# Modulation columns fetched ahead in a two-block transformer kernel, with nine weight buffers, a norm through ones and a bias write from 128 partitions

## The chip, the cores and the metric

The kernel runs on one core of one Trainium2 chip. The metric is the device time of one execution in microseconds (us); the number that counts is the median of several executions.

## What is computed

Two blocks in a row on x of 256 tokens by 2048 channels, all in float32. The first one is modulated by a vector c: six vectors of 2048 (shift, scale and gate for the mixer and for the feed-forward) come from one product with a 2048 x 12288 matrix, `w_ada`.

```python
c_act = jax.nn.silu(c)
mod = c_act @ w_ada[l] + b_ada[l]
sh1, sc1, gt1, sh2, sc2, gt2 = jnp.split(mod, 6, axis=-1)
h = modulate(rms_norm(x, g_mix[l]), sh1, sc1)     # h * (1 + scale) + shift
z = h @ w_in[l]                                   # 2048 -> 11344 columns
...                                               # stick-breaking and top-k sparse attention, with rel_bias
x = x + gt1[:, None, :] * (merged @ w_out[l])
h = modulate(rms_norm(x, g_ffn[l]), sh2, sc2)
a = causal_dwconv(h @ w_gate[l], conv_w[l], conv_b[l])
y = (jax.nn.silu(a) * (h @ w_up[l])) @ w_down[l]
x = x + gt2[:, None, :] * y
```

The second block is gated linear attention and a SwiGLU feed-forward; the change touches it only through the number of weight buffers and one norm.

## The kernel before, in words

Activations are held transposed, 128 channels on the partitions and 256 tokens along the free axis, each as a pair `hi`, `lo` of shorter floats. Every dense layer streams its weights once from memory as **weight tiles** of 128x1024 floats (512 KB). `weights` (L85) takes a buffer `raw`, has SyncE (SP) issue the DMA (L89), lets ScalarE (ACT) round it to `hi` (L92) and VectorE (DVE) take the rest `lo = raw - hi` (L93). There are five `raw` and three `hi` and `lo` buffers. TensorE (PE) then multiplies: three matmuls of 256 columns per 128x128 piece in `mm3` (L120 to L122), 24 per tile, or two (512 and 256 columns) in `dense_b` (L110, L111).

**The modulation is not on TensorE.** `w_ada` is read in 96 **columns** of 128 outputs each, and a column is two `raw` buffers of 512 KB. `mod_col` (L189) issues both DMAs (L196) and has VectorE multiply each with `c_act` and sum along the free axis (L198). The columns share the five `raw` buffers and the SP queue with the weight tiles. Vectors `0` (shift) and `1` (scale) are needed before the first projection can be fed: row block k of h needs column k of both, then `h_mod` (L265 to L274) makes it.

**The first projection, `w_in_k`,** is therefore ordered with the contraction outermost (`batch`, L532): three batches b of 16 output tiles; a batch holds all eight PSUM banks and walks over row blocks k, two weight tiles per step k. Each batch runs in two parts, k from 0 to 6 and from 7 to 15. After the first part ScalarE copies the 16 sums out (L548), after the second VectorE adds them in (L550). `grow` (L525) makes one more row block of h, hence two columns; the function `ahead` says when: every step of the first part of batch 0, every second step later, until all 16 exist in the second part of batch 0. This first stage ends with `w_in_k`; then come `w_in_a` (32 tiles, L163 to L165), `w_in_b` (50), `w_o_dsa` (16), `w_o_sb` (16), `w_out` (32) and the feed-forward.

**The other 64 columns** are spread by a credit: every weight tile adds `self.rate`, and a full credit makes one `mod_step` (L201), fetch and reduction together. The rate is 0.36 from the last two parts of `w_in_k` to the end of `w_o_dsa`, 0 in `w_o_sb` and `w_out`, and 16 columns are left for the feed-forward.

**The first norm** squares x on ScalarE (L495), adds on VectorE (L498), sums over partitions by matmuls with one column each (L501), takes the root (L227) and reciprocal (L228) of 128x2 numbers, and `spread` (L230) brings them back to 128x256 by a diagonal, a matmul (L237) and a copy (L238). `stat_end` (L240) does the same for later norms.

**The bias** of the sparse attention: `rows` (L324) makes 8 rows of 383 numbers on 8 partitions and writes each 128 times to memory as `skew` (L329, 1532 KB); `head` (L332) reads it back with a stride, which shifts each row (L334).

Beside this dense work the attention's steps run from a list, one or two per weight tile (`pump`). A scheduler fixes the order on each engine when the program is built, and each engine and the SP queue works strictly in that order.

Of the kernel before, what the change touches and what calls it, by code (L numbers as in the profile page):

```python
# [32 lines left out]
class Core:  # L33
    def __init__(self, ctx, tc, ap):
# [10 lines left out]
        self.modq = deque()  # L45
        self.rate = self.credit = 0.0
# [38 lines left out]
    def weights(self, src, n):  # L85
# [103 lines left out]
    def mod_col(self, ci, j):  # L189
        nc = self.nc  # L190
        n = ci * KD + j
        m = self.mod[ci][:, j:j + 1]
        for hf in range(2):
            c = slice(hf * 1024, (hf + 1) * 1024)
            raw = self.wp.tile([P, 1024], F32, name="raw", tag="raw", bufs=5)
            nc.sync.dma_start(raw, self.ap["w_ada"][n, :, c])  # L196
            init = m if hf else self.vec["b_ada"][:, n:n + 1]
            nc.vector.tensor_tensor_reduce(out=raw, in0=raw, in1=self.c_act[:, c], scale=1.0, scalar=init,  # L198
                                           op0=ALU.mult, op1=ALU.add, accum_out=m)

    def mod_step(self, n=1):  # L201
        for _ in range(n):
            if self.modq:
                self.mod_col(*self.modq.popleft())

# [33 lines left out]

    def stat_end(self):  # L240
        nc = self.nc
        m = self.misc()
        nq = 4 if self.st_two else 2
        for i, st in enumerate((self.st, self.sq)):
            for q in range(nq):
                nc.tensor.matmul(m[:, q:q + 1], st[:, q * P:(q + 1) * P], self.ones[:, 0:1],
                                 start=(i == 0 and q == 0), stop=(i == 1 and q == nq - 1), skip_group_check=True)
# [4 lines left out]
        self.rs = self.alloc()  # L252
        r1, r2 = self.rs[:, :S], self.rs[:, S:]
        if not self.st_two:
            self.spread(r1, rt[:, :2])
            return r1
# [27 lines left out]
    def setup(self):  # L284
# [7 lines left out]
        self.c_act = self.big()  # L292
        nc.sync.dma_start(self.c_act[0:1, :], ap["c"])
        for i in range(4):
            c = slice(i * 512, (i + 1) * 512)
            m = self.misc()
            nc.tensor.matmul(m, self.ones[0:1, :], self.c_act[0:1, c], start=True, stop=True)
            nc.scalar.activation(self.c_act[:, c], m, AF.Silu)
        self.vec = {}
        off = 0  # L300
        nv = sum(w for _, w in VECS)
        vt = self.cp.tile([P, nv], F32, name="vecs")
        nc.sync.dma_start(vt, ap["vecs"])
        for n, w in VECS:
            self.vec[n] = vt[:, off:off + w]
            off += w
# [7 lines left out]
    # ---- constants of the attention  # L314
    def rel_bias(self):
# [5 lines left out]
        g = self.dp.tile([NH, P, 383], F32, name="skew")  # L321
        self.bias = [self.alloc() for _ in range(4)]

        def rows():  # L324
            m = self.misc()
            nc.tensor.matmul(m[:NH, :383], rb, oh[:32, :383], start=True, stop=True)
            e = self.scr(384)
            nc.scalar.copy(e[:NH, :383], m[:NH, :383])
            nc.sync.dma_start(g, e[:NH, :383].unsqueeze(1).broadcast_to([NH, P, 383]))  # L329
            self.free(oh)  # L330

        def head(h):  # L332
            src = g[h].rearrange("p q -> (p q)")[127:127 + P * 382].rearrange("(p q) -> p q", q=382)[:, :S]
# [143 lines left out]
    def mixer(self):  # L477
# [6 lines left out]
        self.load_consts()  # L484
        sh1, g1 = self.mod[0], self.mod[1]

        def mods(k):
            self.mod_col(1, k)
            self.mod_col(0, k)
            nc.vector.scalar_tensor_tensor(g1[:, k:k + 1], g1[:, k:k + 1], 1.0, self.vec["g_mix"][:, k:k + 1],  # L490
                                           op0=ALU.add, op1=ALU.mult)
        with self.tc.high_priority(offset=400):
            sq = [self.alloc() for _ in xs]
            for j, x in enumerate(xs):
                nc.scalar.activation(sq[j], x, AF.Square)  # L495
            for n in (4, 2, 1):
                for j in range(n):
                    nc.vector.tensor_add(sq[j], sq[2 * j] if n < 4 else sq[j], sq[2 * j + 1] if n < 4 else sq[j + 4])  # L498
            m = self.misc()
            for q in range(4):  # L500
                nc.tensor.matmul(m[:, q % 2:q % 2 + 1], sq[0][:, q * P:(q + 1) * P], self.ones[:, 0:1],  # L501
                                 start=(q == 0), stop=(q == 3), skip_group_check=True)
            self.free(*sq)
            rt = self.sp.tile([P, 4], F32, name="rt", tag="rt", bufs=2)
            self.rstd(rt[:, :2], m[:, :2], D)
            self.rs = self.alloc()
            r = self.rs[:, :S]
# [577 lines left out]
```

## Time and profile before

| | us |
|---|---|
| median of three executions | 2773.17 |
| fastest and slowest of them | 2756.18, 2775.2 |
| span of the profiled execution, first to last instruction | 2767.9 |
| TensorE busy in that span | 2672.7 |

The span stands 5.3 us under the median; which of the executions was profiled isn't told, so what lies around the span is known only as that difference. A profile row of instructions names the line, the engine, the operation, what it writes and reads, the shapes and the count, then busy time, the mean duration, and the idle time before. In a row of time the start comes first, then the duration, and in square brackets how long the engine had been idle and what ended that.

### The profile page before, as it was taken

To read this page: it belongs to the slowest core of one execution; us is meant where nothing else is said; L and a number is where in the kernel's file an instruction comes from. 1 tells how busy PE (TensorE), PEld (TensorE's weight loads), DVE (VectorE), ACT (ScalarE), POOL (GpSimd) and SP (SyncE) were. 2 spreads that over 40 slices of the span, in tenths; PEclk is the share of its full clock that TensorE was granted. 3 is DMA by queue.
4 is the path that set the end of the run, shared out by engine and by line. 5 is a ranking of instruction groups with operands and counts; after the bars stand their busy time and mean duration, and the time that the engine had idled before them with its cause. 6 is when DMAs were issued, how large, how long until landed. Compare 5 with 4: busy or idle time off the path is not lost.

```text
span 2767.9 us, 41793 instructions
## 1 busy us (share of the span) xinstructions
PE 2672.7 (97%) x16310; PEld 2370.0 (86%) x16310; DVE 1876.6 (68%) x2881; ACT 1307.5 (47%) x1929; POOL 0.2 (0%) x4
## 2 busy tenths in 40 slices
PE   6899995999999999999999999999999999999999
PEld 5889874998987888888888888888888888888888
DVE  7886785766768777777655568657766666665444
ACT  3443342554545444444444464445554444444433
POOL 0000000000000000000000000000000000000000
PEclk9999998999999999999999999999999999999999
DMA  8998886877755666666566644545555555556664
GB/s 306 313 327 276 290 270 186 283 240 253 238 190 180 227 221 227 232 216 218 183 181 190 185 158 144 159 152 176 188 184 191 191 189 190 191 190 186 195 204 148
DMA packets 167674, 585.70 MB, mean 212 GB/s; under 512 B 18576, under 2 KB 23408, under 8 KB 167474
## 3 DMA queue, kind: packets, MB, share of 16 engines
q1 hardware_dynamic: 167474, 583.03, 65.1%
q8 instruction: 127, 2.08, 0.3%
q14 instruction: 73, 0.59, 0.1%
HBM read 579.22 MB, written 3.67 MB: 211 GB/s over the span
## 4 chain that ended last, share of the span: by engine, by line
PE 76%; DMA 6%; DVE 4%; issue 2%; ACT 1%; SPq 0%; DVEq 0%; ACTq 0%
PE acc L110 44%; PE acc L111 22%; DMA raw<-in_w_ada 4%; DVE lo L93 2%; PE acc L122 1%; PE acc L120 1%; PE acc L121 1%; PE acc L163 1%; PE acc L164 1%; PE acc L165 1%; DMA raw<-in_w_in_b 1%; DVE raw L198 1%; PE misc L829 1%; DMA raw<-in_w_in_k 1%; ACT hi L92 0%
## 5 line engine op out<-in xcount | busy, mean ns | idle before, releaser
L110 PE MATMUL acc<-slot,hi 128*128 128x512 f32 x5056 | 1775.4, 395 | 1.0 <-DVE t L175 1.0
L93 DVE TENSOR_TENSOR lo<-raw,hi 128x1024 fp32r<-128x1024 f32 (+1 forms) x916 | 1102.9, 1206 | 673.4 <-ACT hi L92 668.5
L92 ACT CAST hi<-raw 128x1024 fp32r<-128x1024 f32 (+1 forms) x916 | 947.0, 1035 | 1217.9 <-issue 544.5
L111 PE MATMUL acc<-slot,lo 128*128 128x256 f32 x5056 | 1420.9, 281 | 0.0
L110 PEld LDWEIGHTS acc<-slot,hi 128*128 128x128 f32 x5056 | 949.2, 188 | 225.2 <-issue 1.5
L111 PEld LDWEIGHTS acc<-slot,lo 128*128 128x128 f32 x5056 | 952.3, 188 | 1.1 <-issue 0.8
L120 PE MATMUL acc<-slot,hi 128*128 128x256 f32 x1056 | 304.5, 290 | 53.5 <-ACT hi L92 49.5
L122 PE MATMUL acc<-slot,lo 128*128 128x256 f32 x1056 | 297.5, 289 | 9.7 <-DVE lo L93 9.1
L121 PE MATMUL acc<-slot,hi 128*128 128x256 f32 x1056 | 300.0, 286 | 0.0
L120 PEld LDWEIGHTS acc<-slot,hi 128*128 128x128 f32 x1056 | 204.0, 193 | 57.7 <-ACT hi L92 52.5
L122 PEld LDWEIGHTS acc<-slot,lo 128*128 128x128 f32 x1056 | 201.2, 194 | 13.8 <-DVE lo L93 13.7
L198 DVE CUSTOM_DVE_ANT_0 raw<-raw,big,vecs 128x1024 f32<-128x1024 f32 x96 | 123.2, 1284 | 125.1 <-DMA raw<-in_w_ada 124.8
L121 PEld LDWEIGHTS acc<-slot,hi 128*128 128x128 f32 x1056 | 204.2, 193 | 0.4 <-DVE slot L273 0.3
L198 DVE CUSTOM_DVE_ANT_0 raw<-raw,big,mod 128x1024 f32<-128x1024 f32 x96 | 123.1, 1283 | 9.6 <-DMA raw<-in_w_ada 8.2
L122 PE MATMUL misc<-slot,lo 128*128 128x256 f32 x384 | 108.2, 282 | 2.5 <-DVE lo L93 2.5
L120 PE MATMUL misc<-slot,hi 128*128 128x256 f32 x384 | 108.5, 283 | 1.6 <-DVE slot L550 1.6
L121 PE MATMUL misc<-slot,hi 128*128 128x256 f32 x384 | 108.2, 282 | 0.0
L163 PE MATMUL acc<-hi,slot 128*128 128x512 f32 x256 | 103.2, 403 | 1.6 <-ACT hi L92 1.3
L164 PE MATMUL acc<-lo,slot 128*128 128x512 f32 x256 | 102.1, 399 | 2.1 <-DVE lo L93 2.1
L165 PE MATMUL acc<-hi,slot 128*128 128x512 f32 x256 | 101.2, 395 | 0.0
L175 DVE TENSOR_TENSOR t<-acc,t 128x256 f32<-128x256 f32 x188 | 78.6, 418 | 0.3
L174 ACT COPY t<-acc 128x256 f32<-128x256 f32 x209 | 76.0, 364 | 1.1 <-PE acc L146 1.1
(223 smaller groups left out, 1744.4 us busy)
## 6 DMA issues: line engine op xcount, KB each, us to landing
raw<-in_w_gu SPq DMA_DIRECT2D x344, 512.0 KB, 3.7
raw<-in_w_ada SPq DMA_DIRECT2D x192, 512.0 KB, 5.4
raw<-in_w_in_k SPq DMA_DIRECT2D x96, 512.0 KB, 5.7
raw<-in_w_down SPq DMA_DIRECT2D x80, 512.0 KB, 4.3
raw<-in_w_dn SPq DMA_DIRECT2D x80, 512.0 KB, 4.5
raw<-in_gla_b SPq DMA_DIRECT2D x66, 512.0 KB, 3.6
raw<-in_w_in_b SPq DMA_DIRECT2D x50, 512.0 KB, 4.8
raw<-in_w_in_a SPq DMA_DIRECT2D x32, 512.0 KB, 4.5
```

What stands on the lines that cost most here:

```text
L92: self.mark = nc.scalar.copy(hi[:, :n], raw[:, :n])
L93: nc.vector.tensor_sub(lo[:, :n], raw[:, :n], hi[:, :n])
L110: nc.tensor.matmul(acc, hi[:, w], x, start=(k + j == 0), stop=False, skip_group_check=True)
L111: nc.tensor.matmul(acc[:, 1], lo[:, w], x[:, 0], start=False, stop=(k + j == kt - 1), skip_group_check=True)
L120: nc.tensor.matmul(out, hi, x[:, 0], start=first, stop=False, **mm)
L121: nc.tensor.matmul(out, hi, x[:, 1], start=False, stop=False, **mm)
L122: nc.tensor.matmul(out, lo, x[:, 0], start=False, stop=last, **mm)
L163: nc.tensor.matmul(o, hs[k][:, 0, tt], hi[:, w], start=(k == 0), stop=False)
L164: nc.tensor.matmul(o, hs[k][:, 0, tt], lo[:, w], start=False, stop=False)
L165: nc.tensor.matmul(o, hs[k][:, 1, tt], hi[:, w], start=False, stop=(k == KD - 1))
L175: nc.vector.tensor_add(out, acc[:, 0], t)
L198: nc.vector.tensor_tensor_reduce(out=raw, in0=raw, in1=self.c_act[:, c], scale=1.0, scalar=init, op0=ALU.mult, op1=ALU.add, accum_out=m)
```

## The change

Five things change together.

- **Fetch and reduction of a column are apart.** `mod_fetch` issues the two DMAs ahead of its place, `mod_reduce` reduces the oldest column fetched. `mod_step` reduces one and fetches the next.
- **Columns come evenly in the first stage:** four columns before the first weight tile, then one fetched and one reduced in every step k of every batch until all 32 are there. The stage runs in three parts for k from 0 to 1 and 2 to 6 (all three batches each) and 7 to 15, so 48 sums more are added in by VectorE. Later the rate is 0.28, and it goes on through `w_o_sb` and `w_out`.
- **Nine `raw` buffers** in place of five.
- **Norms by ones:** the squares go straight into 16 matmuls of 256 columns with a 128x128 matrix of ones, which leaves the sum on every partition; root and reciprocal then run on 128x256. The one-part `stat_end` does so too, with two matmuls.
- **The bias write** has its rows on 128 partitions, 16 copies of each row by the matmul and 8 by the DMA; the bytes are the same.

The rest is order at the start: ScalarE loads the table with Silu at once, x is issued before `vecs`, and `cst` later.

```diff
     def weights(self, src, n):
...
-            raw = self.wp.tile([P, 1024], F32, name="raw", tag="raw", bufs=5)
+            raw = self.raw()
...
-    def mod_col(self, ci, j):
...
+    def mod_fetch(self, offset=120):
+        if not self.modq:
+            return
+        ci, j = self.modq.popleft()
+        raws = []
+        with self.tc.high_priority(offset=offset):
+            for hf in range(2):
+                raws.append(self.raw())
+                self.nc.sync.dma_start(raws[-1], self.ap["w_ada"][ci * KD + j, :, hf * 1024:(hf + 1) * 1024])
+        self.colq.append((ci, j, raws))
+
+    def mod_reduce(self):
...
+    def mod_step(self):
+        if self.colq:
+            self.mod_reduce()
+        self.mod_fetch()
...
+    def token_sums(self, out, parts):
+
+        for i, st in enumerate(parts):
+            self.nc.tensor.matmul(out, self.ones, st, start=(i == 0), stop=(i == len(parts) - 1))
...
+        g = self.dp.tile([P, NH, 383], F32, name="skew")
...
+            nc.vector.tensor_copy(rep[:32, :].rearrange("p (h r) -> p h r", h=NH),
+                                  rb.unsqueeze(2).broadcast_to([32, NH, RP]))
             m = self.misc()
-            nc.tensor.matmul(m[:NH, :383], rb, oh[:32, :383], start=True, stop=True)
+            nc.tensor.matmul(m[:, :383], rep[:32, :], oh[:32, :383], start=True, stop=True)
             e = self.scr(384)
-            nc.scalar.copy(e[:NH, :383], m[:NH, :383])
-            nc.sync.dma_start(g, e[:NH, :383].unsqueeze(1).broadcast_to([NH, P, 383]))
+            nc.scalar.copy(e[:, :383], m[:, :383])
+            nc.sync.dma_start(g, e[:, :383].unsqueeze(1).broadcast_to([P, NH, 383]))
...
+        self.mod_fetch(0)
+        self.mod_fetch(0)
...
+        self.token_sums(m[:, :S], [s[:, h * S:(h + 1) * S] for s in sq for h in range(2)])
...
+                while len(hss) <= k:
+                    column()
...
+                    if half == 0 and len(hss) < KD:
+                        self.mod_fetch()
+                if len(hss) < KD:
+                    column()
...
-        KA = 7
-        batch(0, 0, KA, lambda k: 1)
-        batch(1, 0, KA, lambda k: k % 2)
-        batch(2, 0, KA, lambda k: k % 2)
-        batch(0, KA, KD, lambda k: (k - KA + 1) % 2)
+        self.mod_fetch()
+        self.mod_fetch()
+        for k0, k1 in ((0, 2), (2, 7)):
+            for b in range(3):
+                batch(b, k0, k1)
+        batch(0, 7, KD)
...
-        self.rate = 0.36
+        self.rate = 0.28
...
-        self.rate = 0.0
...
-        self.rate = 0.2 if len(self.modq) > KD else 0.0
```

**On SP, at the start of the first stage.** `raw<-in_w_ada` is half a column, `raw<-in_w_in_k` a weight tile. Before:

```order
11 L311 DMA cst<-in_cst 128x512
12 L196 DMA raw<-in_w_ada 128x1024 x4
13 L89 DMA raw<-in_w_in_k 128x1024 x2
14 L196 DMA raw<-in_w_ada 128x1024 x4
15 L89 DMA raw<-in_w_in_k 128x1024 x2
16 L196 DMA raw<-in_w_ada 128x1024 x4
17 L89 DMA raw<-in_w_in_k 128x1024 x2
18 L196 DMA raw<-in_w_ada 128x1024 x4
```

Changed:

```order
10 L504 DMA vecs<-in_vecs 128x356
11 L201 DMA raw<-in_w_ada 128x1024 x8
12 L93 DMA raw<-in_w_in_k 128x1024
13 L201 DMA raw<-in_w_ada 128x1024 x2
14 L93 DMA raw<-in_w_in_k 128x1024 x2
15 L201 DMA raw<-in_w_ada 128x1024 x2
16 L93 DMA raw<-in_w_in_k 128x1024 x2
17 L201 DMA raw<-in_w_ada 128x1024 x2
18 L93 DMA raw<-in_w_in_k 128x1024 x2
```

Two column halves now stand between two pairs of weight tiles, where four did; the pattern goes on until 64 halves and 55 weight tiles are issued.

**On SP, around the bias write** (`skew<-t` is the write, `slot<-skew` its reads). Before, 130 weight tiles stand ahead of the write:

```order
103 L89 DMA raw<-in_w_in_b 128x1024 x2
104 L329 DMA skew<-t_4380 1024x1x383
105 L196 DMA raw<-in_w_ada 128x1024 x2
106 L89 DMA raw<-in_w_in_b 128x1024 x2
107 L334 DMA slot_3607<-skew 128x256 x2
108 L89 DMA raw<-in_w_in_b 128x1024
```

Changed, 132 stand ahead of it:

```order
117 L93 DMA raw<-in_w_in_b 128x1024 x4
118 L201 DMA raw<-in_w_ada 128x1024 x2
119 L348 DMA skew<-t_4415 1024x1x383
120 L93 DMA raw<-in_w_in_b 128x1024 x2
121 L354 DMA slot_3664<-skew 128x256 x2
122 L354 DMA slot_3665<-skew 128x256 x2
123 L354 DMA slot_3666<-skew 128x256 x2
124 L93 DMA raw<-in_w_in_b 128x1024
```

In both, the copy that the write waits for stands on ScalarE behind the 127th weight tile, and two tiles stand between the write and its first read; the tiles issued ahead of the write went from 130 to 132.

**On VectorE, in `w_o_sb`** (lo is a weight tile's second part, `ISA raw` a column's reduction, the slots are the merge). Before:

```order
789 L93 TENSOR_TENSOR lo<-raw,hi 128x1024
790 L280 SCALAR_TENSOR_TENSOR slot_7342<-slot_195,slot_7342 128x256
791 L629 SCALAR_TENSOR_TENSOR slot_4467<-slot_4467,acc 128x256
792 L630 TENSOR_TENSOR slot_4467<-slot_4467 128x256
793 L93 TENSOR_TENSOR lo<-raw,hi 128x1024
```

Changed:

```order
808 L97 TENSOR_TENSOR lo<-raw,hi 128x1024
809 L300 SCALAR_TENSOR_TENSOR slot_7322<-slot_186,slot_7322 128x256
810 L300 SCALAR_TENSOR_TENSOR slot_7359<-slot_187,slot_7359 128x256
811 L211 ISA raw,mod_80<-raw,big,vecs 128x1024
812 L211 ISA mod_80 128x1
813 L97 TENSOR_TENSOR lo<-raw,hi 128x1024
814 L649 SCALAR_TENSOR_TENSOR slot_4508<-slot_4508,acc 128x256
815 L211 ISA raw,mod_80<-raw,big,mod_80 128x1024
816 L211 ISA mod_80 128x1
```

Reductions now stand between the weight tiles of a stage that had none.

## Rows read from the trace of the kernel before

**Rows 1.** The page: span, TensorE's busy time

```profile
span 2767.9 us, 41793 instructions
...
PE 2672.7 (97%) x16310; PEld 2370.0 (86%) x16310; DVE 1876.6 (68%) x2881; ACT 1307.5 (47%) x1929; POOL 0.2 (0%) x4
```

**Rows 2.** Stretches: length, busy us (instructions) of PE, PEld, DVE, ACT, POOL; clock; DMA; GB/s

```profile
24.00:90.00 66.00, 49.68 (x332) 47.48 (x332) 55.78 (x89) 20.40 (x31) 0.00 (x0) 0.87 0.91 311
90.00:210.00 120.00, 112.54 (x918) 109.33 (x917) 100.26 (x145) 55.35 (x86) 0.00 (x0) 1.00 0.92 320
210.00:343.00 133.00, 126.65 (x1057) 125.31 (x1057) 94.73 (x131) 47.88 (x46) 0.00 (x0) 1.00 0.83 281
454.00:482.00 28.00, 1.59 (x9) 1.21 (x7) 3.24 (x5) 1.86 (x3) 0.00 (x0) 0.61 0.63 141
560.00:720.00 160.00, 149.61 (x1203) 146.71 (x1202) 110.15 (x155) 74.58 (x119) 0.00 (x0) 0.99 0.77 256
720.00:848.00 128.00, 128.00 (x861) 117.92 (x860) 90.48 (x134) 68.56 (x105) 0.00 (x0) 1.00 0.59 193
```

**Rows 3.** ScalarE in order of time, 218 to 226 us

```profile
221.27 1.05 ACT L92 CAST hi<-raw 128x1024 fp32r<-128x1024 f32 x1 [1.79 <-PE misc L121]
224.11 1.05 ACT L92 CAST hi<-raw 128x1024 fp32r<-128x1024 f32 x1 [1.79 <-DMA raw<-in_w_in_k]
225.18 1.28 ACT L558 ACT_TABLE_LOAD   x1
```

**Rows 4.** TensorE in order of time, at the start and at 342.9 us

```profile
2.59 7.16 PE L297 MATMUL misc<-big,ones 1*128 1x512 f32 x8 [2.59 <-DMA big<-in_c]
...
22.97 1.22 PE L120 MATMUL acc<-slot,hi 128*128 128x256 f32 x4 [1.91 <-ACT slot L271]
24.24 0.58 PE L121 MATMUL acc<-slot,hi 128*128 128x256 f32 x1
...
342.89 0.47 PE L163 MATMUL acc<-hi,slot 128*128 128x512 f32 x1 [0.24 <-DVE slot L550]
```

**Rows 5.** SP, TensorE and TensorE's waits around the bias write, in order of time

```profile
441.82 0.81 SPq L329 DMA_DIRECT2D skew<-t  x1
...
476.42 0.81 SPq L334 DMA_DIRECT2D slot<-skew  x2
...
481.37 0.58 PE L120 MATMUL acc<-slot,hi 128*128 128x256 f32 x1 [26.41 <-ACT hi L92]
```

**Rows 6.** Stretches: behind the bias write, behind the hole, and the fastest 10 us

```profile
457.00:475.00 18.00, 0.00 (x0) 0.00 (x0) 0.00 (x0) 0.00 (x0) 0.00 (x0) 0.58 0.57 93
482.00:490.00 8.00, 7.53 (x46) 7.38 (x46) 6.72 (x16) 3.45 (x8) 0.00 (x0) 0.68 0.93 325
170.00:180.00 10.00, 8.97 (x73) 8.57 (x73) 8.34 (x14) 7.68 (x20) 0.00 (x0) 1.00 0.94 347
```

**Rows 7.** TensorE's waits from 560 to 720 us: total, times, longest

```profile
PE acc L122 <- DVE lo L93: 8.7, 6, 2.2
```

**Rows 8.** DMA issues: count, size of one, us from issue to landing

```profile
raw<-in_w_ada SPq DMA_DIRECT2D x192, 512.0 KB, 5.4
...
skew<-t SPq DMA_DIRECT2D x1, 1532.0 KB
```

**Rows 9.** Groups of VectorE's instructions by shape, 0 to 350 us

```profile
L93 DVE TENSOR_TENSOR lo<-raw,hi 128x1024 fp32r<-128x1024 f32 x100 | 121.5, 1224 | 36.3 <-ACT hi L92 34.1 <-DMA raw<-in_w_in_k 1.6
...
L198 DVE CUSTOM_DVE_ANT_0 raw<-raw,big,vecs 128x1024 f32<-128x1024 f32 x45 | 57.7, 1283 | 26.6 <-DMA raw<-in_w_ada 26.5
...
L550 DVE SCALAR_TENSOR_TENSOR slot<-acc,slot 128x256 f32<-128x256 f32 x24 | 8.7, 422 | 0.0
...
L273 DVE TENSOR_TENSOR slot<-t,slot 128x256 fp32r<-128x256 f32 x16 | 6.7, 419 | 0.2 <-ACT slot L271 0.2
```

**Rows 10.** The norm ahead of the feed-forward, in order of time

```profile
851.21 0.17 DVE L228 RECIPROCAL rt<-rt 128x2 f32<-128x2 f32 x1
...
851.95 0.80 PE L237 MATMUL misc<-t,ones 128*128 128x256 f32 x2 [1.07 <-DVE t L236]
```

More of the change, by code (lines that the diff above doesn't have):

```diff
@@ L45, in __init__ @@
         self.modq = deque()
+        self.colq = deque()
         self.rate = self.credit = 0.0
@@ L82, in drain, with raw @@
             self.bg.popleft()()
+    def raw(self):
+        return self.wp.tile([P, 1024], F32, name="raw", tag="raw", bufs=9)
     def weights(self, src, n):
@@ L242, in stat_end @@
         m = self.misc()
-        nq = 4 if self.st_two else 2
+        self.rs = self.alloc()
+        r1, r2 = self.rs[:, :S], self.rs[:, S:]
+        if not self.st_two:
+            self.token_sums(m[:, :S], (self.st[:, :S], self.sq[:, :S]))
+            self.free(self.st)
+            self.rstd(r1, m[:, :S], D)
+            return r1
         for i, st in enumerate((self.st, self.sq)):
-            for q in range(nq):
+            for q in range(4):
                 nc.tensor.matmul(m[:, q:q + 1], st[:, q * P:(q + 1) * P], self.ones[:, 0:1],
-                                 start=(i == 0 and q == 0), stop=(i == 1 and q == nq - 1), skip_group_check=True)
+                                 start=(i == 0 and q == 0), stop=(i == 1 and q == 3), skip_group_check=True)
         self.free(self.st)
@@ L251, in stat_end @@
         self.rstd(rt[:, :2], m[:, :2], D)
[L252 to L256, printed above, removed]
         nc.vector.tensor_mul(rt[:, 2:4], rt[:, :2], rt[:, :2])
@@ L292, in setup @@
         self.c_act = self.big()
+        nc.scalar.preload_act_table_set("silu_and_others")
         nc.sync.dma_start(self.c_act[0:1, :], ap["c"])
[L294 to L298, printed above, removed]
         self.vec = {}
         off = 0
-        nv = sum(w for _, w in VECS)
-        vt = self.cp.tile([P, nv], F32, name="vecs")
-        nc.sync.dma_start(vt, ap["vecs"])
+        self.vt = self.cp.tile([P, sum(w for _, w in VECS)], F32, name="vecs")
         for n, w in VECS:
-            self.vec[n] = vt[:, off:off + w]
+            self.vec[n] = self.vt[:, off:off + w]
             off += w
@@ L483, in mixer @@
             nc.sync.dma_start(xs[k], ap["x"][k])
-        self.load_consts()
+        nc.sync.dma_start(self.vt, ap["vecs"])
         sh1, g1 = self.mod[0], self.mod[1]
[L487 to L498, printed above, removed]
-            m = self.misc()
[L500 to L507, printed above, removed]
-            self.spread(r, rt)
-        mods(0)
+        self.modq.extend((ci, k) for k in range(KD) for ci in (1, 0))
+        self.mod_fetch(0)
+        self.mod_fetch(0)
+        sq = [self.alloc() for _ in xs]
+        for j, x in enumerate(xs):
+            nc.scalar.activation(sq[j], x, AF.Square)
+        for i in range(4):
+            c = slice(i * 512, (i + 1) * 512)
+            m = self.misc()
+            nc.tensor.matmul(m, self.ones[0:1, :], self.c_act[0:1, c], start=True, stop=True)
+            nc.scalar.activation(self.c_act[:, c], m, AF.Silu)
+        m = self.misc()
+        self.token_sums(m[:, :S], [s[:, h * S:(h + 1) * S] for s in sq for h in range(2)])
+        self.free(*sq)
+        self.rs = self.alloc()
+        r = self.rs[:, :S]
+        self.rstd(r, m[:, :S], D)
         kw = self.alloc()
@@ L679, in ffn @@
         nc, ap = self.nc, self.ap
-        while len(self.modq) > KD:
+        while len(self.modq) >= KD:
             self.mod_step()
```

43 lines of the change are left out of this document (21 added, 22 removed).

## The prediction

> **What bounds the kernel now.** I read the page first, then busy time and clock by stretches, then the waits of the stretches that lose time, and last the order of time where a wait began. TensorE is busy 2672.7 of 2767.9 us [rows 1], so at most 95 us of waiting can go, besides time at the lower clock level. In the stretches that the change touches the reader is to see where TensorE stands idle or runs too few matmuls [rows 2].
>
> The measure of a full pace is the time of one weight tile: in an undisturbed row ScalarE starts its casts at 221.27 and 224.11, released by TensorE's matmuls each time, so a tile takes 2.84 us [rows 3], or 24 matmuls in 2.84 us, 8.45 per us. Held against this, the first stage loses 226 of 558 matmuls from 24 to 90 us (26.7 us), 96 of 1014 from 90 to 210 (11.4 us) and 67 of 1124 from 210 to 343 (7.9 us) [rows 2]. That is 46 us, and the whole agrees: the 96 tiles of `w_in_k` need 273 us and take from 24.24 to 342.89, 319 us [rows 4].
>
> The limit there is the DMA. It moves 311 and 320 GB/s at a busy share of 0.91 and 0.92 until 210 us [rows 2], and half a column is as large as a weight tile. At 320 GB/s one 512 KB transfer takes 1.64 us. Until the 32nd column is there, 114 transfers must pass; 114 x 1.64 = 187 us. Only behind that does TensorE set the pace: ScalarE's table load at 225.18 stands behind the 60th tile's cast, and three tiles are then still to be multiplied, so tile 60 ends near 232.6 us [rows 3].
>
> The second place is a hole. The bias write is issued at 441.82, and the first read of it, which waits for its landing, at 476.42 [rows 5]; 34.6 us for 1532 KB [rows 8]. From 457 to 475 us the DMA is busy to 0.57 and moves 93 GB/s [rows 6]. Weights issued behind the write are late, and TensorE waits 26.41 us until 481.37 [rows 5]. The clock then stands at a mean of 0.68 from 482 to 490 us [rows 6], and 0.32 x 8 = 2.6 us more are lost at the lower of its two levels.
>
> The third is small: from 560 to 720 us TensorE waits 8.7 us for `lo`, in six waits [rows 7], and the granted clock of 0.99 costs 1.6 us [rows 2].
>
> **First stage: -13 us.** The bytes stay. Even spreading and nine buffers can only keep the DMA fuller and take work out from behind it. By the new order 64 column halves and 55 weight tiles, 119 transfers, pass until the last column is there. The small loads and x fill the DMA until about 8 us; 119 x 1.64 = 195 us more gives 203. The same count for the kernel before gives 195, which fits a share of 0.92 until 210 us and of 0.83 behind it [rows 2], so I add nothing for startup.
>
> VectorE comes close behind. Per step k it takes two `lo` (2 x 1.22), one column (2 x 1.28), half of an `h_mod` (1.5 x 0.42) and the scalar work: 5.7 us. In the five steps of the middle part the sums are added in, 16 x 0.42 over 5 steps, 1.3 us more: 7.0 [rows 9]. Neighbouring instructions overlap by some 0.1 us each, so about 6.8. The DMA needs 4 x 1.64 = 6.55 per step. In these 15 steps VectorE is 0.25 us slower, 4 us in all: 207. Add 3 us from landing through cast and `lo`, and six tiles that TensorE still has to do, 17 us: tile 60 ends at 227, 6 us earlier than before. The remaining 36 tiles need 102 us at full pace. Before, they took 110; at 0.28 columns per tile the DMA needs 1.56 x 1.64 = 2.56 us per tile and is below TensorE's 2.84, where at 0.36 it needed 2.79. I leave 2 us for changes of banks: the stage ends near 330 in place of 343. The bounds: -28 if the DMA holds its best 10 us, 347 GB/s [rows 6], and 0 if VectorE and the DMA hold each other up as now.
>
> **The start: nothing, bounds -1 and +5.** The four matmuls at 2.59 us hold eight records of 512 columns in 7.16 us [rows 4]; 16 of 256 columns are four times as many matmuls of half the columns, 14.3 us at this pace and half that at the upper clock level, so the norm is ready between 17 and 24 us and the first matmuls come between 24 and 30 (before 22.97, in a row from 24.24 [rows 4]). Nine buffers and eight column halves at the front keep the DMA and VectorE at work meanwhile, which are the limit; that is the cover. Without it the start costs up to 5 us.
>
> The reciprocal now works on 256 numbers per partition where it had 2 in 0.17 us [rows 10]. The nearest row of that shape is 0.42 us [rows 9], and I take that. In the norm ahead of the feed-forward, which is on the path, a matmul of 0.80 us [rows 10] and a copy go, and root and reciprocal grow by some 0.5 together: -0.5 us, which I count as nothing, bounds -1 and +2. The Trainium skill speaks against this part: VectorE: DVE Perf Modes, in its walkthrough of the eight slices, says that the reciprocal divides iteratively, with a repeat count of 8. If each number took eight times as long, an estimate from the 0.42 row is 3.4 us, 3 us more on that path, and the sum below would be 2730; no row here shows it, since the one of 2 numbers is all fixed cost.
>
> **The bias write: -29 us.** The hole's 26.4 and the clock's 2.6. The write's bytes are the same, so its time is bounded by 4.9 us (1532 KB at 320 GB/s) and by half of 34.6, 17.3 us: a busy share near one half fits eight of sixteen engines carrying the write, and twice as many at the same pace halve it. I take something near 8, but both ends are hidden. SP is in order, and what stands behind the write is two tiles and then reads that wait for its landing. When the copy that it needs is done (behind the 127th cast) TensorE is at tile 125, and 132 are issued: eight tiles, 22.7 us, before it needs one from behind the write. At 17.3 us, with 4.5 for the tile behind and 2.3 for cast and `lo`, that is 24.1: a hole of 1.4 us at the upper end, none at the lower.
>
> On this the Trainium skill, DMA: Bandwidth & Descriptors (how a DMA's number of engines is chosen), says that a transfer runs on the largest number of engines up to 16 that divides the outer dimension. Eight partitions give 8, and 128 give 16. The share of 0.57 agrees with the first half; by it alone the write takes the 17.3 us, and the sum is 1.4 us higher.
>
> **From 560 to 720 us: -6 us** of the 8.7 + 1.6, since the DMA needs 2.56 us per tile in place of 2.79. Bounds -10 and +2.
>
> **Columns moved into `w_o_sb` and `w_out`: +2 us.** TensorE is busy all of these 128 us [rows 2]. Per tile 0.56 transfers and 0.28 x 2.6 = 0.7 us of VectorE are added, which has 37 us free there. In VectorE's order a reduction stands close behind the read that frees its buffer, so `lo` may wait for a landing: bounds 0 and +8. The feed-forward has 13 columns left in place of 16 and gains nothing.
>
> **The sum:** -13 - 29 - 6 + 2 = -46 us. Against the span that is 2722; against the median of 2773, 5.3 above it, **2727 us**, 1.7% faster.
>
> **Rivals.** *The DMA gets faster.* Nine transfers may be under way where five were; a 10 us stretch reached 347 GB/s [rows 6], 1.51 us per transfer. Then VectorE's order sets the end of the columns near 195, and the stage gains 12 us more: 2715. Against it: the share is 0.92 already.
>
> *VectorE becomes the bound.* If its 6.8 us per step are paid in all parts, and bank changes wait for its adds behind reductions, the first stage gains nothing: 2740. For it: VectorE is busy 55.8 of 66 us already [rows 2], and the 48 adds are new.
>
> *The write doesn't get faster.* If its pace is set by the many short pieces and not by the engines, it keeps 34.6 us, and with 22.7 us of tiles and 6.8 behind it a hole of about 18 us stays: 2745. Against it: the share of 0.57.
>
> *Slower: the columns hold up `lo`.* After the first stage 51 columns are fetched over 182 tiles, and each reduction stands right behind the release that lets its fetch start, with only one or two `lo` between. A `lo` stays in time through the three buffers, two tiles or 5.7 us ahead, so with 1.3 us for the reduction and 2.84 of spacing a landing of up to some 7.5 us costs nothing. Columns land in 5.4 us now [rows 8], longer only where the DMA is full. From there each us more costs 51 us. If nine buffers lengthened the queue to 9 us, 1.5 x 51 = 77 us are lost: 2804.
>
> **How the numbers follow.** A measurement of this kernel tells about 1% from no change, 28 us; the bound is 2745. The forecast gets 0.56 (its own range 2712 to 2740), the faster DMA 0.14, VectorE as bound 0.13, the slow write 0.12, and the slower case 0.05. The range takes in the first three and most of the fourth: 2704 to 2752. Faster by over 1%: nearly all of the forecast and of the fast DMA, three in four of VectorE's case and half of the slow write's, 0.83; the same 0.12; slower 0.05.
>
> **What would show it.** Right: no wait of TensorE over 3 us near the bias write, and its first read within 18 us of it; `w_in_a` starting near 330; a DMA share over 0.92 up to 205 us; no wait for `lo` in `w_out`. Wrong: a hole of ten us or more behind the write, `w_in_a` starting after 340, VectorE full and the DMA below 0.9 in the middle part, or the landing of columns over 7.5 us.

## The result, and the profile after

Three runs of the changed kernel took 2719.91, 2728.66 and 2736.93 us; a fourth, disturbed one of 3233.41 at a mean clock of 0.752 is left out of all comparisons, and with it the median on record is 2732.8. Against the kernel before, the ratio is 0.9846, 95% interval 0.981 to 0.9882: 1.5% faster, where 2727 us had been forecast. The profiled execution is the one of 2736.93 us. Its page, which answers to [rows 1]:

```profile
span 2735.1 us, 41939 instructions
...
PE 2684.5 (98%) x16320; PEld 2374.2 (87%) x16320; DVE 1882.9 (69%) x2917; ACT 1304.5 (48%) x1925; POOL 0.2 (0%) x4
```

A span 32.8 us shorter does not say where they come from. For that I took from each trace the start of the first matmul of every stage. "Deferred" is an experiment told below.

| from the first matmul of a stage to that of the next, us | before | changed | deferred |
|---|---|---|---|
| start, to the first main matmul | 23.0 | 24.4 | 24.2 |
| `w_in_k` | 319.9 | 293.3 | 288.7 |
| `w_in_a` | 105.6 | 100.3 | 100.3 |
| `w_in_b`, first ten tiles (the hole) | 62.9 | 35.9 | 37.6 |
| `w_in_b`, the rest | 150.7 | 146.4 | 142.5 |
| `w_o_dsa` | 52.4 | 49.8 | 45.4 |
| `w_o_sb` | 45.4 | 50.7 | 45.4 |
| `w_out`, 15 outputs | 83.2 | 97.2 | 85.0 |
| last output, norm, first products of the feed-forward | 39.0 | 39.3 | 38.0 |
| **the feed-forward's repeated matmuls begin at** | **882.0** | **837.2** | **807.1** |
| feed-forward, first two matrices | 474.6 | 474.6 | 465.7 |
| `w_down` | 249.6 | 249.6 | 244.9 |
| `gla_w_out` | 90.6 | 89.0 | 89.0 |
| second block's gate and up | 489.8 | 498.6 | 498.6 |
| `w_dn`, to the last matmul | 243.7 | 248.4 | 248.4 |

Up to the feed-forward the change brings 44.8 us. Behind it, in stages that run the same instructions, 12 us are lost again; that is no wait, and the last section comes back to it.

The stretches of the changed kernel that answer to [rows 2] (columns as there):

```profile
24.00:90.00 66.00, 63.62 (x496) 61.84 (x497) 60.66 (x95) 39.01 (x77) 0.00 (x0) 0.95 0.98 363
90.00:210.00 120.00, 115.40 (x943) 112.22 (x942) 115.50 (x198) 46.44 (x49) 0.00 (x0) 1.00 0.93 340
...
440.00:480.00 40.00, 39.08 (x302) 37.10 (x302) 29.73 (x66) 22.55 (x52) 0.00 (x0) 1.00 0.77 264
650.00:798.00 148.00, 136.92 (x868) 123.08 (x867) 116.79 (x187) 69.34 (x106) 0.00 (x0) 0.97 0.75 258
```

From 24 to 90 us TensorE does 496 matmuls in place of 332, and the DMA moves 363 GB/s in place of 311. From 90 to 210 us VectorE is busy 115.5 of 120 us. From 440 to 480, where the hole was, TensorE is busy 39.08 of 40. But from 650 to 798, `w_o_sb` and `w_out`, it now stands for 11 us and a mean clock of 0.97 costs some 4 more (0.03 x 148), where [rows 2] had it full at 1.00 from 720 on. Its three longest waits from 290 to 830 us (total, times, longest):

```profile
PE acc L126 <- DVE lo L97: 9.8, 7, 2.1
PE acc L149 <- DVE slot L293: 7.2, 1, 7.2
PE acc L115 <- DVE lo L97: 4.8, 2, 3.5
```

All three are for VectorE. Who holds VectorE up is seen in its own waits from 650 to 798 us, and in one of these in order of time, on VectorE, on SP's queue and on TensorE:

```profile
DVE raw L211 <- DMA raw<-in_w_ada: 21.0, 9, 4.9
```

```profile
764.97 0.42 DVE L233 TENSOR_TENSOR slot<-slot,t 128x256 f32<-128x256 f32 x1
770.25 1.28 DVE L211 CUSTOM_DVE_ANT_0 raw<-raw,big,vecs 128x1024 f32<-128x1024 f32 x1 [4.87 <-DMA raw<-in_w_ada]
771.46 0.08 DVE L211 DVE_READ_ACCUMULATOR2_ANT mod<- 128x1 f32 x1
771.46 1.22 DVE L97 TENSOR_TENSOR lo<-raw,hi 128x1024 fp32r<-128x1024 f32 x1
```

```profile
763.09 2.32 SPq L201 DMA_DIRECT2D raw<-in_w_ada  x2
771.57 1.47 SPq L93 DMA_DIRECT2D raw<-in_w_out  x2
```

```profile
772.74 0.58 PE L115 MATMUL acc<-slot,lo 128*128 128x256 f32 x1 [3.46 <-DVE lo L97]
```

The column is issued at 763.09 and lands some 7.2 us later. VectorE has come to its reduction at 765.4 already, waits 4.87 us, and the `lo` behind it is late: TensorE waits 3.46 us for it, until 772.74. SP issues no weight tile until the reduction has ended: the buffers it needs are freed by VectorE. Over the whole stretch from 650 to 798 us SP's issues of weights wait most for reductions:

```profile
SPq L93 <- DVE mod L211: 45.7, 20, 6.1
```

The bias write and the new reciprocal, in order of time on SP and on VectorE:

```profile
407.42 0.61 SPq L348 DMA_DIRECT2D skew<-t  x1
...
418.62 2.71 SPq L354 DMA_DIRECT2D slot<-skew  x6
```

```profile
806.38 1.75 DVE L242 RECIPROCAL slot<-slot 128x256 f32<-128x256 f32 x1 [0.36 <-ACT slot L241]
```

The first read follows the write by 11.2 us (34.6 in [rows 5]). The reciprocal of 256 numbers takes 1.75 us.

### The profile page after: what moved, and what is told of

The parts are those of the page before. It is cut to its first block, busy times and chain, and to the rows that moved or that the text cites. A ratio compares the mean times of both kernels' runs of the same rounds, so it can differ in the third digit from the quotient of the medians.

```text
span 2735.1 us, 41939 instructions
## 1 busy us (share of the span) xinstructions
PE 2684.5 (98%) x16320; PEld 2374.2 (87%) x16320; DVE 1882.9 (69%) x2917; ACT 1304.5 (48%) x1925; POOL 0.2 (0%) x4
## 4 chain that ended last, share of the span: by engine, by line
PE 73%; DMA 1%; DVE 0%; issue 0%; ACT 0%; DVEq 0%
PE acc L114 44%; PE acc L115 22%; PE acc L167 1%; PE acc L168 1%; PE acc L169 1%; PE misc L848 1%; DMA raw<-in_w_ada 1%; PE acc L149 1%; PE acc L150 0%; PE misc L886 0%; DVE lo L97 0%; PE misc L778 0%; PE misc L816 0%; PE misc L888 0%; PE misc L795 0%
## 5 line engine op out<-in xcount | busy, mean ns | idle before, releaser
L114 PE MATMUL acc<-slot,hi 128*128 128x512 f32 x5056 | 1793.4, 398 | 2.2 <-DVE slot L300 2.2
L114 PEld LDWEIGHTS acc<-slot,hi 128*128 128x128 f32 x5056 | 951.1, 188 | 236.7 <-DVE slot L300 2.8
L124 PE MATMUL acc<-slot,hi 128*128 128x256 f32 x1056 | 299.7, 285 | 5.4 <-ACT hi L96 5.4
L125 PE MATMUL acc<-slot,hi 128*128 128x256 f32 x1056 | 297.5, 282 | 1.0 <-DVE slot L293 1.0
L126 PEld LDWEIGHTS acc<-slot,lo 128*128 128x128 f32 x1056 | 199.3, 189 | 11.4 <-DVE lo L97 11.2
L124 PE MATMUL misc<-slot,hi 128*128 128x256 f32 x384 | 105.7, 284 | 1.2 <-ACT hi L96 1.2
L126 PE MATMUL misc<-slot,lo 128*128 128x256 f32 x384 | 98.1, 289 | 7.5 <-DVE lo L97 7.1
L125 PE MATMUL misc<-slot,hi 128*128 128x256 f32 x384 | 104.9, 282 | 0.0
L126 PEld LDWEIGHTS misc<-slot,lo 128*128 128x128 f32 x384 | 67.5, 190 | 11.6 <-DVE lo L97 11.2
```

The lines of the kernel that those rows point to most:

```text
L114: nc.tensor.matmul(acc, hi[:, w], x, start=(k + j == 0), stop=False, skip_group_check=True)
L124: nc.tensor.matmul(out, hi, x[:, 0], start=first, stop=False, **mm)
L125: nc.tensor.matmul(out, hi, x[:, 1], start=False, stop=False, **mm)
L126: nc.tensor.matmul(out, lo, x[:, 0], start=False, stop=last, **mm)
```

## The experiments

Times of whole stretches repeat well: of the changed kernel profiled once more, the feed-forward began at 835.4 in place of 837.2, of the deferred one at 805.9 in place of 807.1. Stages in which TensorE waits repeat less well: in the two profiles of the changed kernel the first ten tiles of `w_in_b` took 35.9 and 39.1 us, `w_o_sb` 50.7 and 49.0, so differences of some 3 us there say nothing. The experiments are read by stage, and totals are given only where several runs stand behind them.

**The new bias write alone, in the kernel before** (b_bias).

```diff
-            nc.tensor.matmul(m[:NH, :383], rb, oh[:32, :383], start=True, stop=True)
+            nc.tensor.matmul(m[:, :383], rep[:32, :], oh[:32, :383], start=True, stop=True)
...
-            nc.sync.dma_start(g, e[:NH, :383].unsqueeze(1).broadcast_to([NH, P, 383]))
+            nc.sync.dma_start(g, e[:, :383].unsqueeze(1).broadcast_to([P, NH, 383]))
```

> The kernel before with the new bias write alone (five buffers, old order of the first stage). Theory (the write was slow because it came from 8 partitions): the first read of the skew buffer follows its write by 11 us, as in the changed kernel, in place of 34.6; the first ten tiles of w_in_b take 35 to 38 us in place of 62.9, and no wait of TensorE there is over 3 us. The first stage ends at 342.9 as before, and the span is 26 to 30 us shorter than before where the matmul pace of the last stages is the same. Rival (the nine buffers are what covers the hole): with five buffers a hole of 10 us or more stays and the ten tiles take over 46 us.

The first read follows the write by 15.0 us, the ten tiles take 41.7 us, and one wait is left:

```profile
PE acc L120 <- ACT hi L92: 4.8, 1, 4.8
```

The write alone takes 21.2 of the 27.0 us. The hole is not quite gone, though I had expected it to be (35 to 38 us, no wait over 3): with five buffers and 0.36 columns per tile 4.8 us stay.

**The old bias write, in the changed kernel** (a_oldbias), the same edit the other way round.

> The changed kernel with the bias written from 8 partitions again. Theory (the write's number of partitions sets its time, and the nine buffers cover only a few tiles of it): the write takes 30 us or more again, TensorE has one long wait of 12 to 20 us (before 26.4; up to four more weight tiles or columns are loaded ahead, some 8 to 11 us), and the first ten tiles of w_in_b take 48 to 58 us in place of 35.9. Rival (buffers cover it): they take under 40 us, and the write was not worth changing beside nine buffers.

```profile
405.56 0.81 SPq L343 DMA_DIRECT2D skew<-t  x1
...
440.40 1.76 SPq L348 DMA_DIRECT2D slot<-skew  x4
```

```profile
PE acc L124 <- ACT hi L96: 14.5, 1, 14.5
```

34.8 us again, and a wait of 14.5; the ten tiles take 51.3. So the rest of the change covers 12 of the 26.4 us (nine buffers alone do as much, as the next experiment shows), and the new write the rest. The write's time goes with its partitions, whatever else is in the kernel: 34.6 to 35.0 us to the first read in all four kernels that write from 8 partitions, 11.2 to 15.2 in all ten profiles of those that write from 128.

**Nine buffers alone, in the kernel before** (b_nine).

```diff
-            raw = self.wp.tile([P, 1024], F32, name="raw", tag="raw", bufs=5)
+            raw = self.wp.tile([P, 1024], F32, name="raw", tag="raw", bufs=9)
```

> The kernel before with nine raw buffers alone (and the smaller DMA scratch that makes room for them). Theory (more transfers under way keep the DMA fuller, and that is where the 25 us of the first stage come from): from 24 to 90 us the DMA rises from 311 to over 345 GB/s, w_in_a starts at 318 to 331 in place of 342.9. Rival (the spread columns and the three parts do it): the DMA stays under 330 GB/s there and w_in_a starts within 4 us of 342.9. The hole behind the old bias write should shrink from 26.4 to 12 to 18 us, as 14.5 remained in the changed kernel with the old write.

The smaller DMA scratch named there is a setting that makes room for the buffers. The changed kernel has it too, beside the five changes listed, and so does a_five below.

```profile
24.00:90.00 66.00, 53.06 (x382) 50.36 (x380) 60.84 (x100) 22.84 (x39) 0.00 (x0) 0.95 0.94 344
```

344 GB/s in place of 311 (I had said over 345), and `w_in_a` starts at 326.6: 16.3 of the 25.2 us. The wait behind the old write is 14.9 us.

**Five buffers in the changed kernel** (a_five), `bufs=9` back to `bufs=5`.

> The changed kernel with five raw buffers, everything else as changed. Theory (buffers): at least half of the 25 us are lost, w_in_a starts at 330 us or later, and the DMA falls under 340 GB/s from 24 to 90 us. Rival (the order): w_in_a starts by 322. Columns in flight take up to four of five buffers here, so weights may be held back: w_in_a beyond 345 would say that the order needs the buffers.

```profile
24.00:90.00 66.00, 61.27 (x461) 58.11 (x462) 57.19 (x89) 36.67 (x74) 0.00 (x0) 0.94 0.93 320
90.00:210.00 120.00, 106.09 (x814) 101.69 (x814) 106.69 (x185) 39.73 (x42) 0.00 (x0) 0.96 0.89 304
```

`w_in_a` starts at 340.6: of 25.2 us only 2.3 are left. The first of these rows is far better than before (461 matmuls, before 332), the second far worse (814, before 918). The new order brings weight tiles forward; that the transfers which it puts off then come due would explain the second row, but was not tested. In the first ten tiles of `w_in_b`, with the new write, no wait is over 1 us (37.1 us for the ten).

**Three parts and an even row of h, in the kernel before** (b_three).

```diff
-        batch(0, 0, KA, lambda k: 1)
-        batch(1, 0, KA, lambda k: k % 2)
-        batch(2, 0, KA, lambda k: k % 2)
-        batch(0, KA, KD, lambda k: (k - KA + 1) % 2)
+        for k0, k1 in ((0, 2), (2, KA)):
+            for b in range(3):
+                batch(b, k0, k1, lambda k: max((step[0] + 1) % 2, k + 1 - len(hss)))
+        batch(0, KA, KD, lambda k: (step[0] + 1) % 2)
```

(`step[0]` counts the steps k over all batches.)

> The kernel before with its first 48 tiles per batch in the three parts of the change and a row block of h made every second step, with five buffers, columns fetched where they are reduced and the old start. Theory (buffers are most of it): w_in_a starts between 336 and 350, since VectorE has 32 of the 48 adds earlier and the DMA is no fuller. Rival (the even spread alone gives it): w_in_a starts by 330.

`w_in_a` starts at 346.6, 3.7 us later than before. By itself the order gains nothing. With nine buffers the other changes together bring 8.9 us more (b_nine ends the stage at 326.6, the changed kernel at 317.7), with five only 2.3 (a_five). How much of the 8.9 is the order was not taken apart.

**Half of the reductions' work left out** (a_halfred). Vectors 0 and 1 are summed over half of their numbers only.

```diff
+        w = 512 if ci < 2 else 1024
...
-            nc.vector.tensor_tensor_reduce(out=raw, in0=raw, in1=self.c_act[:, hf * 1024:(hf + 1) * 1024], scale=1.0,
+            nc.vector.tensor_tensor_reduce(out=raw[:, :w], in0=raw[:, :w], in1=self.c_act[:, hf * 1024:hf * 1024 + w],
```

> The changed kernel in which the reductions of vectors 0 and 1 work on the first 512 of the 1024 numbers of each half column; the other half of these sums is left out, all transfers stay. It takes some 38 us of VectorE's work out of the time until 205 us. Theory (from 90 to 210 us VectorE sets the pace, as it is busy 115.5 of 120 us there, and from 24 to 90 us the DMA at a share of 0.98): the 14th tile starts within 1.5 us of 65.3, the 62nd at 200 to 205 in place of 210.5. Rival (the DMA sets it all the way): the 62nd tile starts at 208.5 or later.

```profile
24.00:90.00 66.00, 62.31 (x496) 60.99 (x497) 49.42 (x94) 39.52 (x77) 0.00 (x0) 0.95 0.99 370
90.00:210.00 120.00, 119.30 (x992) 117.68 (x992) 104.56 (x206) 48.13 (x51) 0.00 (x0) 1.00 0.92 346
```

What the expectation calls the 14th and the 62nd tile are, counted from the stage's first matmul, the 13th and the 61st. The 13th starts at 65.5 us (65.3), the 61st at 204.7 (210.5). So the two stretches have two limits. Up to 90 us less work on VectorE changes nothing, 496 matmuls both times, beside a DMA share of 0.98 and 0.99. From 90 to 210 us the same transfers allow 992 matmuls in place of 943 once VectorE has less to do. TensorE is then busy 119.30 of 120 us: it is the next limit, and so 38 us of VectorE's work bring only 6.

**The old rate of columns** (a_rate).

```diff
-        self.rate = 0.28
+        self.rate = 0.36
...
             self.dense_3(ap["w_o_dsa"][n], NH, ods, gated)
+        self.rate = 0.0
```

> The changed kernel with the old rate of columns: 0.36 per tile until the end of w_o_dsa, then none in w_o_sb and w_out. Theory (columns in these two stages cost the 19 us): w_o_sb falls from 50.7 to 45 to 46.5 us and the 15 outputs of w_out from 97.2 to 82.5 to 85; w_in_a, w_in_b and w_o_dsa get longer by 3 to 12 us together, since a tile there then brings 1.72 transfers. Rival (nine buffers, by longer queues, or the lower clock slow these stages without columns): w_o_sb stays over 49 and w_out over 93.

`w_o_sb` takes 45.4 us and `w_out` 84.8, 17.7 less than in the changed kernel; `w_in_a` to `w_o_dsa` take 340.4 in place of 332.4. Without columns TensorE doesn't stand in these two stages:

```profile
653.00:783.00 130.00, 130.00 (x866) 118.90 (x865) 93.45 (x140) 68.84 (x106) 0.00 (x0) 1.00 0.59 195
```

The columns are the cost. This alone doesn't say whether by their load or by their place.

**The reductions deferred** (a_defer): all fetches stay, and a column's reductions stand behind the current tile's `lo`.

```diff
-            nc.vector.tensor_sub(lo[:, :n], raw[:, :n], hi[:, :n])
+            self.vmark = nc.vector.tensor_sub(lo[:, :n], raw[:, :n], hi[:, :n])
...
         if self.colq:
-            self.mod_reduce()
+            with self.tc.issue_after(self.vmark.ins):
+                self.mod_reduce()
```

What it moves, in VectorE's order with the buffers' numbers. The changed kernel, in which SP issues the column `raw_6647` seven weight tiles after `raw_6440`:

```
774 L211 ISA raw_6647,mod3_80<-raw_6647,big_83,vecs_86 128x1024
775 L211 ISA mod3_80 128x1
776 L97 TENSOR_TENSOR lo_6443<-raw_6440,hi_6442 128x1024
```

Deferred, where SP issues the column `raw_6510` four weight tiles ahead of `raw_6639`:

```
777 L97 TENSOR_TENSOR lo_6642<-raw_6639,hi_6641 128x1024
778 L211 ISA raw_6510,mod3_80<-raw_6510,big_83,vecs_86 128x1024
```

> The changed kernel with each column's two reductions put behind the current tile's lo in VectorE's order (the fetches stay where they are). In the changed kernel's order a reduction stands five to six tiles ahead of its place in the DMA queue. Theory (VectorE waits at a reduction for a column still in flight, and the lo behind it is late): w_o_sb falls from 50.7 to 45 to 47 us and the 15 outputs of w_out from 97.2 to 83 to 87; TensorE's waits for lo from 560 to 830 us fall to under 3 us in all; the whole is 14 to 24 us faster than the changed kernel at the same matmul pace. Rival (the load is too much: VectorE's 0.7 us per tile more, or the DMA's 0.56 transfers): both stages stay within 3 us of 50.7 and 97.2, and the waits go over to the DMA.

`w_o_sb` and `w_out` run from 639 to 769 us here. This stretch, and VectorE's two longest waits in it:

```profile
639.00:769.00 130.00, 130.00 (x862) 118.66 (x862) 117.68 (x188) 68.81 (x106) 0.00 (x0) 1.00 0.86 287
```

```profile
DVE lo L97 <- ACT hi L96: 9.5, 14, 1.4
DVE slot L234 <- ACT t L230: 1.4, 3, 0.5
```

`w_o_sb` takes 45.4 us, `w_out` 85.0, with the columns in them. TensorE does what took 148 us in 130, with no idle time and the clock at 1.00; VectorE has the same work (117.68 us, before the edit 116.79) and the DMA nearly the same bytes. The 21.0 us of waits for `w_ada` are gone, and from 290 to 830 us TensorE waits 0.8 us for `lo`:

```profile
PE acc L126 <- DVE lo L97: 0.8, 1, 0.8
```

So it was the place. In the traces' orders a reduction stands five to seven weight tiles ahead of its column in the changed kernel, in all of these two stages, and three to five behind it here. `w_in_k`, the rest of `w_in_b` and `w_o_dsa` gain some 4 us each as well, so that the whole comes out 30 us earlier at the feed-forward, more than the 14 to 24 expected. The median of four runs is 2699.65 us (2691.66 to 2709.8), 0.9765 of the kernel before (0.9712 to 0.9818). The deferred and the changed kernel were not timed side by side, and their intervals overlap; what sets them apart is the start of the feed-forward, 30 us earlier in both pairs of profiles.

**The old end of the norm on top of it** (a_defer_oldend), `stat_end` as before the change.

```diff
         if not self.st_two:
-            self.token_sums(m[:, :S], (self.st[:, :S], self.sq[:, :S]))
-            self.free(self.st)
-            self.rstd(r1, m[:, :S], D)
+            self.spread(r1, rt[:, :2])
             return r1
```

> The kernel with deferred reductions and with the old end of the one-part norms (sums per token in two columns, root and reciprocal of 2 numbers, spread by a product with a diagonal) in place of the product with ones. Theory (the reciprocal of 256 numbers, 1.75 us, eats what the matmul, the copy and the diagonal gave): from the last copy of the sums to the first row block's product it takes 3.1 to 3.5 us as against 3.5, and from the last column of w_out to the feed-forward's first repeated matmul 37 to 39.5 us as against 38.0. Rival (the new norm saves a microsecond or more): over 39.5 us.

From the last copy to the first scaled row it takes 3.80 us, with the new end 3.50; the stretch from the last output to the feed-forward 37.8 and 38.0. The new end saves 0.3 us on its chain and nothing that is seen behind it. I had it between 3.1 and 3.5: wrong by the same 0.3.

**Less VectorE work per row of h** (a_defer_act).

```diff
-        nc.vector.tensor_scalar(v, u, gc, sc, op0=ALU.mult, op1=ALU.add)
+        if act:
+            nc.scalar.activation(v, u, AF.Identity, bias=sc, scale=gc)
+        else:
+            nc.vector.tensor_scalar(v, u, gc, sc, op0=ALU.mult, op1=ALU.add)
```

> The kernel with deferred reductions, and in the first stage one of the three VectorE instructions of a row block of h (the second scale and shift, 0.41 us) made by ScalarE instead, 0.6 us there. Theory (VectorE sets the pace from 90 to 210 us): 15 x 0.41 = 6 us come off VectorE, and as taking off 38 us there brought 7 us, the 62nd tile starts 1 to 4 us earlier than 210.3. Rival (a row block's delay counts, not VectorE's load): no change within 1 us, or later by up to 3. The median should come out at 2685 to 2705, within what can't be told from 2699.65, and at a ratio of 0.970 to 0.982 to before.

The 61st tile (the expectation's 62nd) starts at 211.4, 1.1 us later. From the 13th to the 61st it is 144.4 us in place of 145.2, but the 13th came 1.9 us later. A miss: 6 us off VectorE bring 0.8 us. The median is 2707.2 us (2706.27 to 2710.75), 0.9763 of before (0.9705 to 0.9821).

**Two kernels profiled again** (after_again, a_defer_again), with no edit.

> The changed kernel once more. Theory (the pace of a pair of matmuls, 0.3467 or 0.3533 us, is not a property of the program but of the execution): until the feed-forward begins all stage starts are within 1.5 us of the first profile's except where TensorE waits for lo (feed-forward begins at 832 to 842), and behind it the stages take one of the two paces each, not necessarily that of the first profile: feed-forward 465.7 or 474.6, gla_w_out 89.0 or 90.6, gate and up 489.8 or 498.6, w_dn 243.7 or 248.4 us. Rival (the program sets the pace): 474.6, 89.0, 498.6 and 248.4 again.

> The kernel with deferred reductions once more. Theory (the pace belongs to the execution): the feed-forward begins within 1 us of 807.1 again, and at least one stage behind it takes the other of its two times (the first profile: feed-forward 465.7, gla_w_out 89.0, gate and up 498.6, w_dn 248.4 us). Rival (the program sets it): all four as before, and a time within 2 us of 2693.5.

The feed-forward's first part took 465.7 us in after_again (474.6 in the first profile) and 474.6 in a_defer_again (465.7). `gla_w_out` took 90.6 us in both, 89.0 in the first profiles. Gate and up and `w_dn` took 498.6 and 248.4 in all four. One detail missed: in a_defer_again the feed-forward began 1.2 us earlier, not within 1.

## Why the prediction was right, and where it was not

The total was right: 44.8 us gained up to the feed-forward, where the sum had 46. But three of its terms were not. Two gave 12 and 5 us more than forecast, one lost 17 more, and that they cancelled is luck. Luck, too, is how close the runs came to 2727: the sum has no term for the 12 us lost behind the feed-forward's start, and the two profiled executions differ by 32.8 us, not 46.

**First stage: -13 forecast, -25.2 measured** (`w_in_a` at 317.7 in place of 342.9). The step that failed is the 1.64 us per transfer, taken from 320 GB/s for the kernel to come as for the one before. "Even spreading and nine buffers can only keep the DMA fuller": that they did, 363 GB/s from 24 to 90 us. In this stage the rival with the faster DMA held, and nearly to the number ("the end of the columns near 195", 12 us more). The last reduction of the 32 columns ends at 195.0, where the sum had 207:

```profile
193.73 1.28 DVE L211 CUSTOM_DVE_ANT_0 raw<-raw,big,mod 128x1024 f32<-128x1024 f32 x1
```

Counted as the sum counts, its 119 transfers took at most 1.56 us each (193.73 - 8, over 119). Tile 60 ends at 210.5, forecast at 227. The count for the kernel before was off the other way: it gave 195, but there SP issues the last half only at 194.9, and its reduction ends at 202.1.

b_nine and a_five show the cause: buffers. 16.3 of the 25.2 us come with nine buffers alone, 2.3 with everything but the buffers, and the other 6.6 only with both. VectorE as the limit was right as well, but only from 90 to 210 us, where a_halfred gains some 6 us.

**The start: nothing (-1 to +5), +1.5** (the first matmul at 24.43 in place of 22.97). The run of main matmuls begins at 26.00 in place of 24.24 us.

**`w_in_a`: nothing, -5.3.** I had left it out of the sum. It isn't the rate: a_rate, with the old one, takes 100.7 us there. It doesn't need the buffers: a_five takes 100.3, though nine buffers alone bring 2.1 (103.5 in b_nine). What is left is the fetch apart from the reduction, or the new order before it; these were not tried singly.

**The bias write: -29, -27.0.** The write's time, near 8 us with bounds of 4.9 and 17.3, is 11.2 to 15.2 us up to its first read. Halving had been worked out with each engine's pace unchanged, and that was not so: in the traces the write is 1024 packets of 1532 bytes either way, which took 0.20 to 0.22 us each from 8 partitions and 0.11 to 0.13 from 128. Equal pieces at another pace also rule out the rival in which the pieces set it. The Trainium skill's rule on a DMA's number of engines (DMA: Bandwidth & Descriptors, how the number is chosen) gave an estimate of 17.3 us by halving; the runs agree in direction, and the gain is larger than half. With the write alone a wait of 4.8 us stays; it is gone with the other changes and five buffers (a_five), and with nine buffers and the old rate one of 3.8 us for `lo` is left (a_rate).

**From 560 to 720 us: -6, -6.9** (rest of `w_in_b` and `w_o_dsa`). TensorE's waits for `lo` in these stages fell from 8.7 to 3.6 us, the way that was forecast. The 2.79 us per tile at the old rate should have been 2.82 (1.72 x 1.64), which changes nothing.

**Columns in `w_o_sb` and `w_out`: +2 (0 to +8), +19.2.** This is the step that failed most. I had written that a `lo` stays in time through three buffers and "a landing of up to some 7.5 us costs nothing" (its own terms give 7.2), with the reduction right behind the release that lets its fetch start. The median landing of a column is 5.3 us, and it cost 19 us all the same. The order shows why: a reduction stands in front of the `lo` of a tile whose transfer was issued seven weight tiles earlier than the column's. VectorE arrives there before the column, every wait also holds up the buffers from which the next weights are issued, and a tile's slack is used up at once. The forecast's slower rival had this mechanism, with a threshold that was too high. a_defer shows the cause by taking it away: fetches and work stay, the place alone changes, and the 19 us go but for 1.8. These 1.8 aren't the columns': `w_out` takes 84.8 us in a_rate too, and in three kernels made from the one before, where the profile before had 83.2.

**The norm: -0.5, -0.3 on its chain.** The reciprocal was taken at 0.42 us and measured at 1.75. The Trainium skill (VectorE: DVE Perf Modes, the walkthrough of the eight slices) has a repeat count of 8, from which an estimate of 3.4 was made; the measurement lies between, at 4.2 times the row of 0.42. The copies and the matmul that went paid for it.

Of the signs named ahead, the hole, the first read and the DMA share came as said. `w_in_a` came 12 us earlier than "near 330", and "no wait for `lo` in `w_out`" was wrong.

## What to carry to other kernels

Where one engine works on two streams in a fixed order, find for every wait in it how far its transfer stands behind the work next to it in the DMA queue; a fetch far ahead is worth nothing if the instruction that uses it was moved ahead as far. Count the buffers before the bytes: with 512 KB transfers, five and nine buffers were 311 and 344 GB/s in the same order of work. And where a total comes out right, look at its terms: here an error of 17 us on one side was hidden by 12 and 5 on the other.

## What the runs showed that was not expected

**Two paces of the same matmuls.** In stages that repeat a pair of matmuls (512 and 256 columns) a pair takes 0.3467 or 0.3533 us from a stage's beginning to its end, at a granted clock of 1.00 and with no wait between. The changed kernel's two profiles, line L114 from 900 to 1290 us:

```profile
900.00:1290.00 390.00, 390.00 (x1105) 207.19 (x1104) 1.00 0.64 213
```

```profile
900.00:1290.00 390.00, 390.00 (x1127) 211.08 (x1126) 1.00 0.65 217
```

1105 and 1127 pairs in the same 390 us, and "busy" shows full both times: only the count tells. In the feed-forward (8.9 us, and 4.7 in `w_down`) the pace changes from one execution of the same program to the next; it is no part of the change. Between the deferred kernel's two profiles it makes the difference: 2693.49 and 2707.31 us, some 13.5 of it in these two stages. Nor is it the chip: on each of two chips both paces came up. In gate and up and `w_dn` it was the faster pace in all four profiles of kernels made from the one before and the slower in all ten of those made from the changed one, 13.5 us in all. That may be a cost of the change. Neither the nine buffers, the new write nor the three parts bring it when made alone, and neither the old write, five buffers, the old rate nor the old end of the norm takes it away; the start, the place of the constants and the fetches apart were not tried singly, and the cause stays open.

**The DMA goes higher than the best 10 us before suggested.** From 180 to 200 us the changed kernel moves 409 GB/s, where [rows 6] had 347:

```profile
180.00:200.00 20.00, 19.73 (x164) 19.52 (x165) 19.07 (x29) 9.00 (x10) 0.00 (x0) 1.00 1.03 409
```
